# A hand-set order for the first loads and splits of x in a hybrid state-space / convolution step

## The chip, the cores and the metric

The kernel runs on one core of a Trainium2 chip. The metric is the time on the device in microseconds (us); a kernel's time is the median of several executions.

## The reference

The reference is one inference step of a two-layer decoder trunk, for a prompt of 512 tokens and 64 tokens of samples that share all weights. Cut to what matters:

```python
xn = rms_norm(x, norm_mix[0])                  # x: tokens x 1024
proj = xn @ w_in_ab                            # columns z | x,B,C | dt (Mamba-2) and u (S5)
ya = mamba2_mixer(proj[..., :A_PROJ], ...)     # causal conv, chunked scan, gate
yb = s5_mixer(proj[..., A_PROJ:], ...)         # 64 groups of 16 channels, complex diagonal state, GLU
x = x + concatenate([ya, yb]) @ w_out_ab
x = x + square(relu(rms_norm(x, norm_ff[0]) @ w_ff1[0])) @ w_ff2[0]
x = x + conformer_conv_module(rms_norm(x, norm_mix[1]), ...)
x = x + square(relu(rms_norm(x, norm_ff[1]) @ w_ff1[1])) @ w_ff2[1]
y = rms_norm(x, norm_final)                    # all in float32
```

## The kernel before

**Layout.** All 576 tokens run together. x lies with its 1024 channels on the partitions, as eight tiles of 128 x 576 (channels by tokens), named xi0 to xi7. A weight is read in tiles of 128 output columns: one DMA brings 128 x 1024, which holds eight blocks of 128 x 128, one for each tile of x.

**Products.** A float32 product is made of three products of a shorter format: each operand is split into hi (rounded, on ScalarE) and lo (the remainder, on VectorE). `load` (L203 to L213) does so for a weight tile: the DMA is issued on SyncE (L208), hi is written by ScalarE (L211) and lo by VectorE (L212). Its pool has two buffers. `mm` (L215) then issues for each of the eight blocks hi by hi, hi by lo and lo by hi, each for two halves of 288 tokens: 48 matmuls a tile (L226), into one of two PSUM buffers; a buffer (its "bank" below) comes free when the tile has been read out. `split_scaled` (L243) splits x with the norm's weight multiplied in, hi as fxh on ScalarE (L248) and lo as fxl on VectorE (L249).

**The norm.** The scale of each token is not multiplied into x but into the products. `tok_sum` (L263) squares the tiles on ScalarE (L270; the first is named sa, the others sq), adds them up on VectorE (L274) and sums over the channels on TensorE (tsum, L280). `rstd_tok` (L283) makes the scale r on VectorE by three Newton steps (last step L298), and `bcast_tok` (L300) spreads r over the partitions by small matmuls (bc, L310), which ScalarE copies out as rB (L311, L312).

**The first mixer.** `mixer0` (from L1043) loads x (L1051), splits it, makes the norm's scale, then the S5 coefficients (`s5_coef`: many small steps on VectorE, polynomial steps at L418, products at L509) and tables (`s5_in`: kt by TensorE, L559; ks = kt + dm by VectorE, L562; transposes p, L568). Eight tiles of w_in follow, tiles 0 to 7, for the S5 inputs u. Tiles 0 and 1 are copied out raw by ScalarE (ur, L1066); tiles 2 to 7 are read from PSUM by VectorE when it multiplies by rB to make u (`s5_u`, L576), which is written to memory and read back for the state products (s5s, L600). Tile 8 is dt. Then come four groups of six tiles, tiles 9 to 32, for the convolution, the scan and the gate of Mamba-2 (first step on VectorE: xb, L757), while the S5 outputs are made beside them. The output projection follows, whose residual sum is xr (L1138).

**What sets the order.** Each engine works off its own queue in program order and waits for the other engines by semaphores. The order in a queue is made when the kernel is built: a scheduler takes the next instruction by a modelled time line and a priority. `with self.hp(...)` raises the priority of what is recorded inside; `load` is recorded so, with 3000. Of the loads of x only xi0 is raised (4000):

```python
for k in range(8):
    t = self.X("xi%d" % k)
    with self.hp(4000 if k < 1 else 0):
        nc.sync.dma_start(t, I["x"][k])
    x.append(t)
act = [self.split_scaled(x[k], self.v("nm0", k), "fx", self.B) for k in range(8)]
_, rB = self.rms(x, "rB0")
```

Two small loads are issued from ScalarE's own queue: aco, the convolution's state (L727), and adt, the bias and decay of dt (L733).

Of the kernel before, what the change touches and what calls it, by code (L numbers as in the profile page):

```python
# [1 line left out]

# [1 line left out]

# [4 lines left out]
F32 = mybir.dt.float32  # L9
F32R = mybir.dt.float32r  # L10
AF = mybir.ActivationFunctionType
ALU = mybir.AluOpType
# [130 lines left out]
class Build:  # L143
# [46 lines left out]
    def consts(self):  # L190
# [8 lines left out]
        self.ident, self.tri, self.tris, self.same = (c[:, i * 128:(i + 1) * 128] for i in range(4))  # L199
        self.m8, self.md, self.sgn = c[:, 512:520], c[:, 520:536], c[:, 536:537]  # L200


    def load(self, src, eng=None):  # L203
        nc = self.nc
        eng = eng or nc.vector
        with self.hp():
            raw = self.wp.tile([128, 1024], F32, tag="raw", name="raw")
            nc.sync.dma_start(raw, src)  # L208
            hi = self.wp.tile([128, 1024], F32R, tag="hi", name="hi")
            lo = self.wp.tile([128, 1024], F32R, tag="lo", name="lo")  # L210
            nc.scalar.activation(hi, raw, AF.Copy)  # L211
            eng.tensor_tensor(lo, raw, hi.bitcast(F32), op=ALU.subtract)  # L212
        return hi, lo  # L213

    def mm(self, src, act, eng=None, halves=(0, 1)):  # L215

        nc = self.nc
        hi, lo = self.load(src, eng)
        ps = self.pm.tile([128, 2, 512], F32, tag="mm", name="mm")
        n = 0  # L220
        for kb in range(8):
            ah, al = act[kb]
            k = slice(kb * 128, kb * 128 + 128)
            for w, a in ((hi, ah), (hi, al), (lo, ah)):
                for h in halves:
                    nc.tensor.matmul(ps[:, h, :H], w[:, k], a[:, h * H:(h + 1) * H], start=n == 0, stop=n == 23)  # L226
                n += 1
        return ps[:, :, :H]
# [34 lines left out]
    def tok_sum(self, tiles, mk=None, mk2=None, bank=None):  # L263

        nc = self.nc
        mk = mk or (lambda n: self.tp.tile([128, NT], F32, tag="sa", name=n, bufs=1))
        acc = None
        for t in tiles:
            s = ((mk2 or self.t)("sq") if acc is not None else mk("sa"))[:, :t.shape[-1]]
            nc.scalar.activation(s, t, AF.Square)  # L270
            if acc is None:
                acc = s
            else:
                nc.vector.tensor_tensor(acc, acc, s, op=ALU.add)  # L274
        n = acc.shape[-1]
        c, p = n // 128, n % 128
        ps = (bank or self.bank)("tsum")
        for k in range(c + 1):
            m = 128 if k < c else p
            nc.tensor.matmul(ps[:m, k:k + 1], acc[:, k * 128:k * 128 + m], self.ones[:, 0:1], start=True, stop=True)  # L280
        return ps, c, p
# [761 lines left out]
    def mixer0(self):  # L1043
        nc, I = self.nc, self.I
        with self.tc.tile_pool(name="q1", bufs=5) as self.q1, ExitStack() as inner:
            self.qs = inner.enter_context(self.tc.tile_pool(name="qs", bufs=2))
            x = []
            for k in range(8):
                t = self.X("xi%d" % k)
                with self.hp(4000 if k < 1 else 0):  # L1050
                    nc.sync.dma_start(t, I["x"][k])  # L1051
                x.append(t)
            act = [self.split_scaled(x[k], self.v("nm0", k), "fx", self.B) for k in range(8)]
            _, rB = self.rms(x, "rB0")
            self.s5_coef()
            self.a_conv_init()
            self.S = self.qs.tile([128, 72, 2, 32], F32, tag="S", name="S", bufs=1)
# [1 line left out]
            for m in range(2):  # L1059
                P[m] = self.s5_in(m)  # L1060
            for m in range(8):
                ps = self.mm(I["w_in"][m], act)
                if m < 2:
                    t = self.t("ur", "t")
                    with self.hp():
                        nc.scalar.activation(h2(t), ps, AF.Copy)  # L1066
                    ps = h2(t)
# [65 lines left out]
            for m in range(8):  # L1133
                ps = self.mm(I["w_out"][8 + m], act)
# [284 lines left out]
```

## Time and profile before

| | |
|---|---|
| three executions | 1676.21, 1678.60, 1682.48 us |
| median | 1678.6 us |
| profiled execution, its own time | 1674.24 us |
| span of its trace | 1672.5 us |
| TensorE's granted clock, mean over the span | 0.970 of full speed |
| TensorE busy (matmuls) | 1591.3 us, 95% of the span |
| VectorE busy | 1054.5 us, 63% |
| ScalarE busy | 634.8 us, 38% |
| instructions | 28815 |

The durations of the rows come from the one profiled execution. Its own time is 1.74 us longer than its span, and 4.4 us shorter than the median of the three executions. The busy shares are means over the whole span: they say which engine is closest to full, but not which one is waited for in a given stretch. That is read from the timelines, where a row gives start, length, engine, line, operation, output<-inputs, shape, and in square brackets the idle time of the engine just before and what ended it. A row with "x4" stands for four instructions in a row.

### The profile page before, as it was taken

Reading aid. Unit: us, or ns where it says so; the run is one execution under the profiler, and the core shown is the slowest. Engines: PE = TensorE matmul, PEld = TensorE weight load, DVE = VectorE, ACT = ScalarE, POOL = GpSimd, SP = SyncE. Lnnn points to the kernel's source line nnn. Section 1 sums busy time; section 2 is a strip of 40 time slices with the busy share of each in tenths; the row PEclk is TensorE's granted clock in tenths of the full one; section 3 lists DMA queues with packets and bytes.
Section 4 is the critical chain, followed back from the end, with each engine's and each line's share of the span. In section 5 each row is a group of like instructions: output and inputs, shape, how many; then the busy total and the mean of one; then the engine's idle time right before and its main releaser. Section 6 shows DMA issues by size and latency. Waiting matters only on the chain.

```text
span 1672.5 us, 28815 instructions
## 1 busy us (share of the span) xinstructions
PE 1591.3 (95%) x11833; PEld 1557.6 (93%) x11833; DVE 1054.5 (63%) x1796; ACT 634.8 (38%) x1081; POOL 4.7 (0%) x45
## 2 busy tenths in 40 slices
PE   7999889999998999999999999996799999999997
PEld 7999789989897999999999999995799999999996
DVE  7988899876647966754443557587454443444466
ACT  4244556675514333322222353223333222222244
POOL 0000000000000000000000000000000000000000
PEclk9999999999998999999999999997799999999998
DMA  6644457687766434432222245641022222222234
GB/s 197 180 109 132 131 172 197 197 267 220 251 234 188 94 97 129 154 127 78 87 77 88 78 146 148 189 107 30 25 77 77 89 76 89 85 81 88 78 127 132
DMA packets 149883, 214.43 MB, mean 128 GB/s; under 512 B 59034, under 2 KB 94874, under 8 KB 149752
## 3 DMA queue, kind: packets, MB, share of 16 engines
q1 hardware_dynamic: 146088, 211.28, 41.2%
q8 instruction: 93, 1.52, 0.4%
q10 hardware_dynamic: 3664, 1.32, 0.3%
q14 instruction: 38, 0.31, 0.1%
HBM read 181.22 MB, written 31.34 MB: 127 GB/s over the span
## 4 chain that ended last, share of the span: by engine, by line
PE 82%; DVE 7%; DMA 6%; ACT 2%; issue 1%; SPq 1%; ACTq 0%; DVEq 0%
PE mm L226 72%; PE pc L1308 2%; DVE lo L212 1%; DMA sg<-cumd 1%; DMA rl<-yad 1%; PE pc L1374 1%; PE tsum L1216 1%; PE bc L310 1%; DMA rl<-ybd 1%; DMA rl<-yg 1%; PE pt L1259 1%; DMA ud<-u 1%; PE s5s L600 1%; PE s5y L704 0%; PE s5y L705 0%
## 5 line engine op out<-in xcount | busy, mean ns | idle before, releaser
L211 ACT ACTIVATE hi<-raw 128x1024 fp32r<-128x1024 f32 x217 | 229.7, 1060 | 740.2 <-PE mm L226 685.6
L226 PE MATMUL mm<-fxh,hi 128*128 128x288 f32 x1920 | 418.2, 299 | 23.8 <-ACT hi L211 10.4
L212 DVE TENSOR_TENSOR lo<-raw,hi 128x1024 fp32r<-128x1024 f32 x217 | 264.8, 1221 | 259.0 <-ACT hi L211 257.5
L226 PE MATMUL mm<-fxh,lo 128*128 128x288 f32 x1920 | 417.4, 298 | 0.0
L226 PE MATMUL mm<-fxl,hi 128*128 128x288 f32 x1920 | 415.0, 298 | 0.0
L226 PEld LDWEIGHTS mm<-fxh,hi 128*128 128x128 f32 x1920 | 311.7, 190 | 26.7 <-ACT hi L211 12.7
L226 PEld LDWEIGHTS mm<-fxh,lo 128*128 128x128 f32 x1920 | 311.6, 190 | 1.8 <-issue 1.1
L226 PEld LDWEIGHTS mm<-fxl,hi 128*128 128x128 f32 x1920 | 311.9, 190 | 0.4
L226 PE MATMUL mm<-gh,hi 128*128 128x288 f32 x1024 | 230.0, 295 | 0.0
L226 PE MATMUL mm<-gh,lo 128*128 128x288 f32 x1024 | 229.4, 295 | 0.5 <-DVE lo L212 0.5
L226 PE MATMUL mm<-gl,hi 128*128 128x288 f32 x1024 | 229.5, 295 | 0.0
L226 PEld LDWEIGHTS mm<-gh,lo 128*128 128x128 f32 x1024 | 167.5, 188 | 0.8 <-DVE lo L212 0.8
L226 PEld LDWEIGHTS mm<-gl,hi 128*128 128x128 f32 x1024 | 167.9, 188 | 0.0
L226 PEld LDWEIGHTS mm<-gh,hi 128*128 128x128 f32 x1024 | 167.6, 188 | 0.0
L350 DVE TENSOR_TENSOR fft<-mm,r2B 128x576 f32<-128x576 f32 x56 | 42.4, 758 | 140.5 <-PE mm L226 140.5
L1376 DVE SCALAR_TENSOR_TENSOR acc<-hb,vec,acc 128x512 f32<-128x512 f32 x104 | 77.2, 748 | 1.3
L343 DVE TENSOR_TENSOR ffr<-ffr 128x576 f32<-128x576 f32 x64 | 48.5, 758 | 2.3 <-ACT gh L342 0.4
L344 DVE TENSOR_TENSOR gl<-ffr,gh 128x576 fp32r<-128x576 f32 x64 | 48.5, 758 | 2.1
L342 ACT ACTIVATE gh<-ffr 128x576 fp32r<-128x576 f32 x64 | 44.1, 689 | 2.0
L351 DVE TENSOR_TENSOR x<-x,fft 128x576 f32<-128x576 f32 x56 | 42.4, 758 | 1.8
L765 DVE SCALAR_TENSOR_TENSOR cvo<-xb,vh,cvo 128x600 f32<-128x600 f32 x48 | 40.0, 833 | 1.4 <-ACT cvo L763 1.4
L340 ACT ACTIVATE ffr<-mm 128x576 f32<-128x576 f32 x64 | 40.6, 634 | 0.0
(356 smaller groups left out, 1903.1 us busy)
## 6 DMA issues: line engine op xcount, KB each, us to landing
raw<-w_ff SPq DMA_DIRECT2D x136, 512.0 KB, 3.5
raw<-w_in SPq DMA_DIRECT2D x33, 512.0 KB, 3.7
raw<-w_pw SPq DMA_DIRECT2D x24, 512.0 KB, 3.6
dm<-dwm SPq DMA_DIRECT2D x16, 576.0 KB, 5.9
h<-ass SPq DMA_DIRECT2D x16, 512.0 KB, 4.7
raw<-w_out SPq DMA_DIRECT2D x16, 512.0 KB, 4.5
U<-ud SPq DMA_DIRECT2D x16, 288.0 KB, 3.0
xsd<-xs SPq DMA_DIRECT2D x16, 288.0 KB, 4.0
```

Of the source, the lines that this page charges most:

```text
L211: nc.scalar.activation(hi, raw, AF.Copy)
L212: eng.tensor_tensor(lo, raw, hi.bitcast(F32), op=ALU.subtract)
L226: nc.tensor.matmul(ps[:, h, :H], w[:, k], a[:, h * H:(h + 1) * H], start=n == 0, stop=n == 23)
L340: nc.scalar.activation(h2(r), ps, AF.Relu)
L342: nc.scalar.activation(hi, r, AF.Square)
L343: nc.vector.tensor_tensor(r, r, r, op=ALU.mult)
L344: nc.vector.tensor_tensor(lo, r, hi.bitcast(F32), op=ALU.subtract)
L350: nc.vector.tensor_tensor(h2(t), ps, rB, op=ALU.mult)
L351: nc.vector.tensor_tensor(x[m], x[m], t, op=ALU.add)
L765: nc.vector.scalar_tensor_tensor(o[:, 0:600], xb[:, k:k + 600], self.half("acw", 16 * k + m), o[:, 0:600], op0=ALU.mult, op1=ALU.add)
L1308: nc.tensor.matmul(pc[:, g * 128:g * 128 + 128], w[:, j * 128:j * 128 + 128], hq[:, g, j:j + 128], start=j == 0, stop=j == 8)
L1376: nc.vector.scalar_tensor_tensor(ap, hb[:, k:k + NP], w(k), ap, op0=ALU.mult, op1=ALU.add)
```

## The change

The eight tiles of x and of their splits are now taken from their pools first. Then, all with priority 4000, each tile is loaded, rounded on ScalarE and its remainder made on VectorE; the load and the split of weight tile 0 are recorded right behind those of xi0, and `mm` takes this tile as already loaded. The loads are kept as one list (SyncE), the roundings as another (ScalarE) and the remainders as a third (VectorE), with those of weight tile 0 in second place. Behind the list of ScalarE stands the first square, and behind that of VectorE the first add of squares. `chain` ties each instruction of a list to the one ahead of it, as an order for the scheduler, without a semaphore. `tok_sum` keeps its squares and adds for that. What is computed stays the same. (`behind_load`, which is also new, is called nowhere and is left out below; the line numbers of the new kernel are higher by 13 from `load` on and by 22 behind this place in `mixer0`.)

```diff
--- before
+++ after
...
+    def chain(self, ins):
+
+        for a, b in zip(ins, ins[1:]):
+            self.tc.add_manual_dep(b.ins, a.ins.name, mybir.DependencyInfo(mybir.DependencyClass.NoSync, mybir.DependencyReason.DATA),
+                                   reason="chain")
+
...
     def load(self, src, eng=None):
         nc = self.nc
         eng = eng or nc.vector
         with self.hp():
             raw = self.wp.tile([128, 1024], F32, tag="raw", name="raw")
-            nc.sync.dma_start(raw, src)
             hi = self.wp.tile([128, 1024], F32R, tag="hi", name="hi")
             lo = self.wp.tile([128, 1024], F32R, tag="lo", name="lo")
-            nc.scalar.activation(hi, raw, AF.Copy)
-            eng.tensor_tensor(lo, raw, hi.bitcast(F32), op=ALU.subtract)
+            self.last = [nc.sync.dma_start(raw, src), nc.scalar.activation(hi, raw, AF.Copy),
+                         eng.tensor_tensor(lo, raw, hi.bitcast(F32), op=ALU.subtract)]
         return hi, lo
 
     def mm(self, src, act, eng=None, halves=(0, 1)):
 
         nc = self.nc
-        hi, lo = self.load(src, eng)
+        hi, lo = src if isinstance(src, tuple) else self.load(src, eng)
         ps = self.pm.tile([128, 2, 512], F32, tag="mm", name="mm")
         n = 0
         for kb in range(8):
@@ -264,14 +277,14 @@
 
         nc = self.nc
         mk = mk or (lambda n: self.tp.tile([128, NT], F32, tag="sa", name=n, bufs=1))
-        acc = None
+        acc, self.sq = None, ([], [])
         for t in tiles:
             s = ((mk2 or self.t)("sq") if acc is not None else mk("sa"))[:, :t.shape[-1]]
-            nc.scalar.activation(s, t, AF.Square)
+            self.sq[0].append(nc.scalar.activation(s, t, AF.Square))
             if acc is None:
                 acc = s
             else:
-                nc.vector.tensor_tensor(acc, acc, s, op=ALU.add)
+                self.sq[1].append(nc.vector.tensor_tensor(acc, acc, s, op=ALU.add))
         n = acc.shape[-1]
         c, p = n // 128, n % 128
         ps = (bank or self.bank)("tsum")
@@ -1044,14 +1057,23 @@
         nc, I = self.nc, self.I
         with self.tc.tile_pool(name="q1", bufs=5) as self.q1, ExitStack() as inner:
             self.qs = inner.enter_context(self.tc.tile_pool(name="qs", bufs=2))
-            x = []
-            for k in range(8):
-                t = self.X("xi%d" % k)
-                with self.hp(4000 if k < 1 else 0):
-                    nc.sync.dma_start(t, I["x"][k])
-                x.append(t)
-            act = [self.split_scaled(x[k], self.v("nm0", k), "fx", self.B) for k in range(8)]
+
+            x = [self.X("xi%d" % k) for k in range(8)]
+            act = [(self.B("fxh", F32R), self.B("fxl", F32R)) for k in range(8)]
+            q = [[], [], []]
+            with self.hp(4000):
+                for k in range(8):
+                    q[0].append(nc.sync.dma_start(x[k], I["x"][k]))
+                    q[1].append(nc.scalar.activation(act[k][0], x[k], AF.Copy, scale=self.v("nm0", k)))
+                    q[2].append(nc.vector.scalar_tensor_tensor(act[k][1], x[k], self.v("nm0", k), act[k][0].bitcast(F32),
+                                                               op0=ALU.mult, op1=ALU.subtract))
+                    if k == 0:
+                        w0 = self.load(I["w_in"][0])
+                        for a, b in zip(q, self.last):
+                            a.append(b)
             _, rB = self.rms(x, "rB0")
+            for a, b in zip(q, ([], self.sq[0], self.sq[1])):
+                self.chain(a + b[:1])
             self.s5_coef()
             self.a_conv_init()
             self.S = self.qs.tile([128, 72, 2, 32], F32, tag="S", name="S", bufs=1)
@@ -1059,7 +1081,7 @@
             for m in range(2):
                 P[m] = self.s5_in(m)
             for m in range(8):
-                ps = self.mm(I["w_in"][m], act)
+                ps = self.mm(I["w_in"][m] if m else w0, act)
                 if m < 2:
                     t = self.t("ur", "t")
                     with self.hp():
```

The scheduler then orders the rest anew, so more moves than the diff names. Three places follow.

**The start, ScalarE and TensorE.** fxh is the rounding of a tile of x (xi_90 is xi0 in both; then every second number before, every number after, up to xi7), hi that of a weight tile, sq and sa the squares; aco and adt are the small loads. ScalarE before, from the load adt on:

```order
L727 DMA aco<-acs 128x16x24
L733 DMA adt<-adt 128x32
L211 ACTIVATE hi<-raw 128x1024 x2
L248 ACTIVATE fxh<-xi_92,vec 128x576
L270 ACTIVATE sq<-xi_92 128x576
L754 ACTIVATE xb<-aco 128x8x3
L248 ACTIVATE fxh<-xi_94,vec 128x576
L270 ACTIVATE sq<-xi_94 128x576
L827 ACTIVATE ea<-adt 128x16
L248 ACTIVATE fxh<-xi_96,vec 128x576
```

ScalarE in the new order, from the same load on:

```order
L746 DMA adt<-adt 128x32
L224 ACTIVATE hi<-raw 128x1024
L1067 ACTIVATE fxh<-xi_91,vec 128x576
L283 ACTIVATE sq<-xi_91 128x576
L1067 ACTIVATE fxh<-xi_92,vec 128x576
L283 ACTIVATE sq<-xi_92 128x576
L767 ACTIVATE xb<-aco 128x8x3
L1067 ACTIVATE fxh<-xi_93,vec 128x576
L283 ACTIVATE sq<-xi_93 128x576
L840 ACTIVATE ea<-adt 128x16
L1067 ACTIVATE fxh<-xi_94,vec 128x576
L1067 ACTIVATE fxh<-xi_95,vec 128x576
```

Weight tile 1's rounding, which stood with tile 0's in the row "x2", has moved behind all roundings of x; xi6 and xi7 follow the last row shown, then sa, the square of xi0, and then two weight tiles. The loads aco and adt stand ahead of the first weight rounding in both.

TensorE's first rows before; mm_526 is tile 0 and mm_659 tile 1:

```order
L226 MATMUL mm_659<-fxh_106,hi_655 128x288 x2
L226 MATMUL mm_659<-fxl_107,hi_655 128x288 x2
L226 MATMUL mm_526<-fxh_110,hi_522 128x288 x2
L226 MATMUL mm_659<-fxh_106,lo_656 128x288 x2
L226 MATMUL mm_659<-fxh_110,hi_655 128x288 x2
L226 MATMUL mm_526<-fxl_111,hi_522 128x288 x2
L226 MATMUL mm_526<-fxh_110,lo_523 128x288 x2
```

and in the new order, at the same rows:

```order
L239 MATMUL mm_526<-fxh_100,hi_118 128x288 x2
L239 MATMUL mm_526<-fxl_101,hi_118 128x288 x2
L239 MATMUL mm_526<-fxh_100,lo_119 128x288 x2
L239 MATMUL mm_526<-fxh_102,hi_118 128x288 x2
L239 MATMUL mm_526<-fxl_103,hi_118 128x288 x2
L239 MATMUL mm_526<-fxh_102,lo_119 128x288 x2
L239 MATMUL mm_526<-fxh_104,hi_118 128x288 x2
```

Tile 1 was woven into tile 0; now it starts in row 25, when all rows of tile 0 are done.

**VectorE around r.** r is the norm's scale; the rows at L418 before are polynomial steps of the S5 coefficients, those at L509 (L522 after) products. Before:

```order
L296 TENSOR_TENSOR rs<-ry 128x5
L418 SCALAR_TENSOR_TENSOR wr_195<-wr_195,wr_196 128x96 x2
L418 SCALAR_TENSOR_TENSOR wr_196<-wr_196 128x96
L297 TENSOR_TENSOR rs<-rs,rv 128x5
L418 SCALAR_TENSOR_TENSOR wr_195<-wr_195,wr_196 128x96 x2
L418 SCALAR_TENSOR_TENSOR wr_196<-wr_196 128x96
L298 SCALAR_TENSOR_TENSOR r_167<-rs,ry 128x5
L289 MEMSET rv 128x1
L418 SCALAR_TENSOR_TENSOR wr_195<-wr_195,wr_196 128x96 x2
L434 SCALAR_TENSOR_TENSOR mag<-wr_195,ei 128x96
```

In the new order:

```order
L309 TENSOR_TENSOR rs<-ry 128x5
L487 TENSOR_TENSOR AR<-pw 128x96
L522 TENSOR_TENSOR wr_202<-wr_202 128x96
L522 TENSOR_TENSOR wr_201<-wr_202,wr_201 128x96
L490 TENSOR_TENSOR pw<-AI,AR 128x96
L522 TENSOR_TENSOR wr_201<-wr_201 128x96
L310 TENSOR_TENSOR rs<-rs,rv 128x5
L485 TENSOR_TENSOR pw<-AR 128x192
L426 TENSOR_SCALAR wr_202<-wr_202 128x96
L491 TENSOR_TENSOR AI<-pw 128x96
L311 SCALAR_TENSOR_TENSOR r_173<-rs,ry 128x5
```

r has moved from row 81 to row 114: the steps of the S5 coefficients that stand ahead of it are more, and include the reciprocal and the first powers (pw, AR, AI), which stood behind it. bc follows tile 2 and stands ahead of tile 3 in TensorE's queue in both orders.

**VectorE around u.** u of tiles 0 and 1 is made from ur, that of tile 2 from the PSUM bank mm, which comes free by it. Before:

```order
L212 TENSOR_TENSOR lo<-raw,hi 128x1024
L455 SCALAR_TENSOR_TENSOR wr_195<-wr_196 128x96
L418 SCALAR_TENSOR_TENSOR wr_195<-wr_195,wr_196 128x96
L576 TENSOR_TENSOR u<-ur,rB_185 128x72x8
L509 TENSOR_TENSOR wr_195<-wr_195 128x96
L509 TENSOR_TENSOR wr_196<-s5c 128x96
L418 SCALAR_TENSOR_TENSOR wr_195<-wr_195,wr_196 128x96
L576 TENSOR_TENSOR u<-ur,rB_185 128x72x8
L413 TENSOR_SCALAR wr_196<-wr_195 128x96
L418 SCALAR_TENSOR_TENSOR wr_195<-wr_195 128x96
L509 TENSOR_TENSOR wr_196<-s5c 128x96
L576 TENSOR_TENSOR u<-mm,rB_185 128x72x8
```

In the new order:

```order
L589 TENSOR_TENSOR u<-ur,rB_191 128x72x8
L487 TENSOR_TENSOR AR<-pw 128x384
L491 TENSOR_TENSOR AI<-pw 128x384
L566 TENSOR_TENSOR bb<-bb,bt 128x128
L589 TENSOR_TENSOR u<-ur,rB_191 128x72x8
L507 TENSOR_SCALAR L_318<-AR 128x32 x2
L564 TENSOR_TENSOR bs<-by,kr 128x128
L507 TENSOR_SCALAR L_318<-AI 128x32 x2
L508 TENSOR_SCALAR AI<-AI,cst 128x9x64
L565 TENSOR_TENSOR bt<-bx,kis 128x128
L547 TENSOR_TENSOR G<-AR,bb 128x1024
L589 TENSOR_TENSOR u<-mm,rB_191 128x72x8
```

u of tile 2 stood in row 98, 17 rows behind r; it now stands in row 143, 29 rows behind r, with the powers of A (L485 to L491 of the new kernel) and the first product for G (L547) ahead of it.

## Rows read from the trace of the kernel before

**Rows 1.** The page: busy us, share of the span and instructions of each engine
```profile
PE 1591.3 (95%) x11833; PEld 1557.6 (93%) x11833; DVE 1054.5 (63%) x1796; ACT 634.8 (38%) x1081; POOL 4.7 (0%) x45
```

**Rows 2.** Stretches: start:end, length, busy PE, PEld, DVE, ACT, POOL; granted clock, DMA share, GB/s
```profile
150.00:290.00 140.00, 124.06 (x930) 119.32 (x930) 133.87 (x280) 78.03 (x179) 1.07 (x9) 0.94 0.54 161
290.00:400.00 110.00, 105.54 (x839) 100.01 (x838) 83.09 (x159) 73.80 (x187) 0.20 (x2) 0.97 0.77 234
```

**Rows 3.** ScalarE's timeline: start us, us, engine line op, out<-in [idle before <-releaser]
```profile
5.05 4.18 ACTq L733 DMA_DIRECT2D adt<-adt  x1
...
9.27 2.00 ACT L211 ACTIVATE hi<-raw 128x1024 fp32r<-128x1024 f32 x2 [2.39 <-issue]
...
16.59 0.76 ACT L248 ACTIVATE fxh<-xi,vec 128x576 fp32r<-128x576 f32 x1
...
17.26 0.67 ACT L270 ACTIVATE sq<-xi 128x576 f32<-128x576 f32 x1
```

**Rows 4.** SyncE's timeline, the last seven loads of x
```profile
2.12 6.99 SPq L1051 DMA_DIRECT2D xi<-x  x7
```

**Rows 5.** TensorE's timeline, at twelve places of the first 270 us
```profile
10.38 0.85 PE L226 MATMUL mm<-fxh,hi 128*128 128x288 f32 x2 [10.38 <-ACT hi L211]
...
14.69 0.69 PE L226 MATMUL mm<-fxl,hi 128*128 128x288 f32 x2
...
15.17 0.69 PE L226 MATMUL mm<-fxh,lo 128*128 128x288 f32 x2
...
17.14 0.43 PE L226 MATMUL mm<-fxh,lo 128*128 128x288 f32 x2
...
17.41 0.42 PE L226 MATMUL mm<-fxl,hi 128*128 128x288 f32 x2
...
25.94 1.15 PE L280 MATMUL tsum<-ones,sa 128*128 128x1 f32 x10
...
33.98 1.52 PE L310 MATMUL bc<-cst,r 128*128 128x128 f32 x10 [0.15 <-DVE rv L289]
...
36.48 0.53 PE L226 MATMUL mm<-fxh,hi 128*128 128x288 f32 x2 [0.98 <-ACT ur L1066]
...
42.98 0.42 PE L226 MATMUL mm<-fxh,hi 128*128 128x288 f32 x2
...
80.24 0.66 PE L568 MATMUL p<-cst,G 128*128 128x128 f32 x4 [2.59 <-DVE ks L562]
...
131.93 0.38 PE L226 MATMUL mm<-fxh,lo 128*128 128x288 f32 x1
...
263.93 0.51 PE L226 MATMUL mm<-fxh,hi 128*128 128x288 f32 x2
```

**Rows 6.** VectorE's timeline, at seven places up to 486 us
```profile
33.77 0.15 DVE L298 SCALAR_TENSOR_TENSOR r<-rs,ry 128x5 f32<-128x5 f32 x1
...
34.53 0.25 DVE L418 SCALAR_TENSOR_TENSOR wr<-wr,wr 128x96 f32<-128x96 f32 x1
...
34.70 1.22 DVE L212 TENSOR_TENSOR lo<-raw,hi 128x1024 fp32r<-128x1024 f32 x1
...
39.36 1.32 DVE L576 TENSOR_TENSOR u<-mm,rB 128x576 f32<-128x576 f32 x1
...
130.84 0.29 DVE L562 TENSOR_TENSOR ks<-kt,dm 128x128 f32<-128x128 f32 x1 [4.65 <-PE kt L559]
...
264.68 0.21 DVE L757 TENSOR_TENSOR xb<-mm,rB 128x64 f32<-128x64 f32 x1
...
485.32 0.76 DVE L1138 TENSOR_TENSOR xr<-mm,xr 128x576 f32<-128x576 f32 x1 [1.99 <-PE mm L226]
```

**Rows 7.** Stretches of 2 us, columns as in rows 2: the first matmuls, and 80 to 84
```profile
14.00:16.00 2.00, 2.00 (x10) 2.00 (x10) 2.00 (x7) 1.40 (x4) 0.00 (x0) 1.00 0.98 317
...
80.00:82.00 2.00, 1.76 (x11) 1.74 (x12) 2.00 (x4) 0.60 (x1) 0.00 (x0) 0.71 0.56 130
...
82.00:84.00 2.00, 2.00 (x11) 1.65 (x11) 1.99 (x3) 0.81 (x2) 0.00 (x0) 0.50 0.93 298
```

More of the change, by code (lines that the diff above doesn't have):

```diff
@@ L1 @@
-from contextlib import ExitStack
+from contextlib import ExitStack, contextmanager
 import numpy as np
@@ L200, in consts, with behind_load @@
         self.m8, self.md, self.sgn = c[:, 512:520], c[:, 520:536], c[:, 536:537]
+    def chain(self, ins):
+        for a, b in zip(ins, ins[1:]):
+            self.tc.add_manual_dep(b.ins, a.ins.name, mybir.DependencyInfo(mybir.DependencyClass.NoSync, mybir.DependencyReason.DATA),
+                                   reason="chain")
+    @contextmanager
+    def behind_load(self):
+        with ExitStack() as st:
+            for i in self.last:
+                st.enter_context(self.tc.issue_after(i.ins))
+            yield
     def load(self, src, eng=None):
```

## The prediction, made before the result was known

> **What bounds the kernel now.** I read the page's busy shares first, then the stretches, then the timelines of the engines over the first 50 us and at a few later points. TensorE is busy 95% of the span [rows 1], so an edit wins only where TensorE stands still or runs slowly, and loses by adding such places. One such place is the start: the first matmul comes at 10.38 us [rows 5]. Another is 150 to 290 us: TensorE is busy 124.1 of 140 us and VectorE 133.9 [rows 2]. There VectorE sets the pace, and TensorE stands still for 15.9 us.
>
> The start is held by ScalarE. The issue of the small load adt stands in its queue from 5.05 to 9.23, and only behind it does the first weight split run, 9.27 on [rows 3]. TensorE then has work without a gap until the sums of squares at 25.94 [rows 5].
>
> **The start after the change.** The squares and w1 go behind the x splits, but adt's issue stays ahead of the first weight split on ScalarE, as the order shows. So the first matmul stays at 10.4 and the loads in front gain nothing there. SyncE issued the last x before 9.11 [rows 4] and now does so one weight issue sooner; ScalarE reaches those tiles later anyway, so I cost that at nothing. If ScalarE were free sooner, the same loads would be what it waits for next.
>
> Before, tiles 0 and 1 of w_in were woven together; now tile 0 runs alone. ScalarE does seven more roundings and three squares, 0.67 us start to start [rows 3], before x7 is rounded: 10.3 + 10 times 0.67 and two short steps give about 17.5. VectorE's remainder of x7 follows at about 19.2, and tile 0 ends at 19.8. Tile 1 then waits for its own weight remainder, which VectorE does behind all x remainders: 20.3 plus 1.2 [rows 6] gives 21.5, and 44 matmuls at 0.134 [rows 5] end at 27.4 against 25.94. That is **1.5 us late**.
>
> Here the clock is to be weighed. The matmuls before 16 us stand 0.24 us apart, those behind 0.134 [rows 5]; 288 columns make 0.24 at 1.2 GHz and 0.12 at 2.4. I let the slow pace stay for the same stretch, since TensorE stood idle before it in both kernels. But the granted clock reads 1.00 there [rows 7]; if that is right and the pace is only the weave waiting for splits, tile 0 alone loses it and 24 times 0.106 = 2.5 us come back. The Trainium skill (TensorE: Matmul & The Clock Gate, section "What's actually happening") puts it so: "the default state is throttled, and activity releases the throttle"; by that page nothing comes back, and the sum stands without it.
>
> **The step that I think decides: the row scale.** The scale r of the first norm is written on VectorE at 33.77 before [rows 6], just as TensorE ends tile 2, and its broadcast bc starts at 33.98 [rows 5]. In the new order 107 VectorE instructions lie from the first weight remainder to r, where there were 73. The 34 more are one weight remainder (1.2), 7 polynomial steps (0.17 each start to start, as from 34.53 to 34.70 [rows 6]), 11 products of the same size, a reciprocal (0.7) and 14 of 0.1 to 0.3: about 7.2 us. VectorE waits a little for tile 3's split and for the sums there, as it did before for a split, so r comes at 41.0.
>
> bc stands in TensorE's queue ahead of tile 3 in both orders. Tile 2 with the sums (1.1 us) ends at 27.4 + 6.4 + 1.1 = 34.9, so TensorE stands still about 6 us. From bc to tile 3 it took 36.48 - 33.98 = 2.5 us [rows 5], because ScalarE empties tile 1's bank only behind the broadcast; tile 3 starts at 43.6. Tile 4 needs tile 2's bank, which u frees. That u began at 39.36 [rows 6]; the new order puts 12.0 us more of VectorE's work ahead of it (the 7.2, then the powers of A and the first product for G). It ends at 39.36 + 12.0 + 1.3 = 52.7, and tile 4 starts there, against 42.98 [rows 5]: **9.7 us late**. Every tile of w_in behind it is late with it.
>
> **What comes back.** VectorE does the S5 coefficients in that time, so the small S5 matmuls (kt, p2, s5s) now run between tiles 4 to 8 and not behind them. Before, TensorE needed 131.93 - 42.98 = 88.95 us [rows 5] from tile 4 until nearly all of these and three conv tiles (9 to 11) were done, 2.6 of it a wait for ks [rows 5]. Without that wait and the three tiles (144 matmuls at 0.134 = 19.3) the work is 67.0. In the new order it is done at 52.7 + 67.0 = 119.7, and with the three tiles at 139.0, against 131.93: **7 us late** is left. VectorE's last S5 step stood at 130.84, behind a wait of 4.65 [rows 6]; it now has two conv tiles less ahead of it (some 10 us), so it is done by about 115, and the late side is TensorE.
>
> Then comes the stretch where VectorE sets the pace. TensorE's 7 us could vanish in its 15.9 us of standing still [rows 2], which gives 0. Against that: when VectorE had done its work up to 264.68 (xb of tile 24) [rows 6], TensorE was starting tile 26, at 263.93 [rows 5]. In the new order, with as much work done on VectorE, TensorE starts tile 23. Three tiles less and 1.4 us more of small matmuls: 17.9 us of TensorE's work have left VectorE's shadow. VectorE comes to that point at about 258 (the same work less 1.6, and some 5 us less waiting, as the 4.65 goes). The rest took 485.32 - 264.68 = 220.6 us [rows 6]; it grows by about 20 for that work and shrinks by about 6, for a late TensorE no longer meets the last wait before 290 nor most of the 4.5 us at 290 to 400 [rows 2]. 258 + 220.6 + 20 - 6 = 492.6 against 485.3: +7. From there on the order differs in detail only, and I count nothing.
>
> The ends of this step are 0 and +10 (if VectorE does not wait less). I take **+7**, the end that counts the work row by row and that agrees with the lateness at 131.93. Against the profiled execution (1674.24) that is 1681. The median of the runs is 1678.6, 4.4 above it, and 1678.6 + 7 = 1685.6, so I say 1685. About 0.5% (8.4 us) is what a measurement of this kernel can tell from no change.
>
> **Rivals.**
> Slower: the same late r, but nothing is repaid. The two gaps between 35 and 53 each put the array on the lower clock: after the wait of 2.59 us that ends at 80.24 [rows 5] the granted clock is 0.71 and 0.50 until 84 [rows 7], 1.6 us lost each time, 3.2 for both. And VectorE waits again for a kt, which now stands near the end of tile 7's matmuls: 4.65, as before [rows 6]. 10 + 3.2 + 4.65 = +18, so 1696. It decides from the point where TensorE still stands still 13 us or more at 150 to 290. For it: VectorE's queue order is fixed, so r cannot come sooner. Against: a VectorE that runs on while TensorE is late has less left to do.
>
> Faster: TensorE's 15.9 us of standing still vanish, because S5 is off VectorE 15 us sooner: 7 - 15.9 = -8.9, so 1670, or 1667 if the 2.5 us of the slow start come back too. For it: VectorE is the pacer there. Against: two conv tiles are merely moved behind.
>
> No effect: the change does not do what it says, since adt and not the loads holds the first matmul, and the late r is swallowed whole by later waits: 1679. For it: 15.9 us of waits are more than 9.7.
>
> **How the numbers follow.** Forecast (+7) 0.40, slower rival 0.32, faster 0.12, no effect 0.16. Four fifths of the forecast's own spread (+2 to +10) lie within the bound. So faster 0.12, same 0.16 + 0.32 = 0.48, slower 0.32 + 0.08 = 0.40. The range runs from the faster rival, 1667, to 3 us above the slower one, 1699.
>
> **What would show it.** Right: first matmul at 10.2 to 10.6; sums of squares at 31 to 33; bc at 40 to 42 with TensorE idle about 6 us ahead of it; tile 4 at 51 to 55; the last kt before 120; granted clock under 1 between 35 and 60. Wrong at the first step if the first matmul comes before 9.5, at the second if bc starts before 37, at the third if TensorE stands still less than 6 us at 150 to 290, which would make the kernel faster.

## The result: 16.6 us slower, and the profile after

| | before | after |
|---|---|---|
| median of 6 runs, us | 1683.0 | 1698.5 |
| lowest and highest, us | 1676.2, 1684.9 | 1695.3, 1701.5 |
| ratio to before | | 1.0099 [1.0076, 1.0123] |
| profiled execution, span, us | 1672.5 | 1699.7 |
| granted clock, mean of the span | 0.970 | 0.955 |

The changed kernel is 1.0% slower; on the 1678.6 us of the prediction that is +16.6 us, for a forecast of +7. (The ratio is one of means; the two medians differ by 15.5 us.) The two profiled executions lie at opposite ends of their kernels' runs, so their spans differ by 27.2 us: I use them to find places, and the ratios for sizes.

The page after, its line on busy engines, beside [rows 1]:

```profile
PE 1606.4 (95%) x11833; PEld 1571.7 (92%) x11833; DVE 1056.1 (62%) x1796; ACT 634.0 (37%) x1081; POOL 4.6 (0%) x45
```

TensorE has the same 11833 matmuls, but is busy 1606.4 - 1591.3 = 15.1 us longer. It also stands still longer: 1699.7 - 1606.4 = 93.3 us for 1672.5 - 1591.3 = 81.2. So about half of the difference of the spans is standing still, and about half is matmuls that run slower. Both have places. TensorE's timeline after, at the start:

```profile
9.89 0.85 PE L239 MATMUL mm<-fxh,hi 128*128 128x288 f32 x2 [9.89 <-ACT hi L224]
...
15.16 0.68 PE L239 MATMUL mm<-fxl,hi 128*128 128x288 f32 x2
...
15.64 0.47 PE L239 MATMUL mm<-fxh,lo 128*128 128x288 f32 x2
...
30.80 1.15 PE L293 MATMUL tsum<-ones,sa 128*128 128x1 f32 x10
...
40.70 2.69 PE L323 MATMUL bc<-cst,r 128*128 128x128 f32 x10 [5.90 <-DVE rv L302]
...
44.25 0.85 PE L239 MATMUL mm<-fxh,hi 128*128 128x288 f32 x2 [0.86 <-ACT ur L1088]
```

and VectorE's, with the scale r, the u of tile 2, and the two waits for kt (columns of both as in [rows 3]):

```profile
40.48 0.17 DVE L311 SCALAR_TENSOR_TENSOR r<-rs,ry 128x5 f32<-128x5 f32 x1
...
50.60 1.32 DVE L589 TENSOR_TENSOR u<-mm,rB 128x576 f32<-128x576 f32 x1
...
111.64 0.29 DVE L575 TENSOR_TENSOR ks<-kt,dm 128x128 f32<-128x128 f32 x1 [5.23 <-PE kt L572]
...
119.67 0.29 DVE L575 TENSOR_TENSOR ks<-kt,dm 128x128 f32<-128x128 f32 x1 [2.79 <-PE kt L572]
```

bc comes at 40.70 behind 5.90 us of standing still, for 0.15 in [rows 5], since VectorE writes r at 40.48 and not at 33.77 [rows 6]. Then stretches of after, columns as in [rows 2]:

```profile
0.00:267.80 267.80, 231.44 (x1669) 223.13 (x1670) 231.53 (x527) 125.35 (x269) 1.34 (x15) 0.91 0.54 153
...
39.00:50.00 11.00, 8.44 (x34) 8.03 (x35) 11.00 (x42) 1.36 (x3) 0.24 (x2) 0.53 0.27 74
...
150.00:290.00 140.00, 124.56 (x924) 119.30 (x923) 132.99 (x272) 79.46 (x184) 0.90 (x9) 0.90 0.58 167
...
380.00:401.00 21.00, 16.50 (x82) 16.24 (x81) 15.01 (x28) 12.31 (x25) 0.00 (x0) 0.52 0.78 240
...
527.00:545.00 18.00, 11.05 (x43) 10.04 (x44) 13.06 (x18) 6.68 (x10) 0.15 (x1) 0.53 0.80 203
```

and of before, the first 264.68 us and the last two of these:

```profile
0.00:264.68 264.68, 236.53 (x1788) 229.45 (x1789) 231.48 (x531) 126.69 (x272) 1.56 (x17) 0.97 0.54 156
...
380.00:401.00 21.00, 21.00 (x158) 20.35 (x157) 12.14 (x26) 13.73 (x35) 0.00 (x0) 0.92 0.79 234
...
527.00:545.00 18.00, 14.71 (x94) 13.84 (x93) 14.70 (x16) 6.22 (x8) 0.15 (x1) 0.91 0.37 89
```

The granted clock is 0.53 of full speed in the 11 us around the late bc, 0.52 and 0.53 in the two later stretches, where before it was 0.92 and 0.91 (the same time, somewhat later work). Each such stretch has a wait in it or just ahead of it. TensorE's waits after, summed up over the first 600 us (what waits, what for: us in all, times, longest; without the wait for the first weight):

```profile
PE mm L239 <- ACT yah L261: 12.7, 4, 5.6
...
PE yps L937 <- DVE ya L949: 8.6, 2, 8.2
...
PE yoff L979 <- DMA h<-ass: 6.0, 3, 4.5
...
PE bc L323 <- DVE rv L302: 5.9, 1, 5.9
...
PE cum L850 <- DVE da L842: 4.4, 1, 4.4
```

and before:

```profile
PE scr L898 <- ACT bt L890: 4.6, 1, 4.6
...
PE mm L226 <- DVE z L779: 4.1, 1, 4.1
...
PE tsum L280 <- DVE sa L274: 3.1, 1, 3.1
...
PE p L568 <- DVE ks L562: 2.6, 1, 2.6
...
PE mm L226 <- ACT yah L248: 2.6, 3, 1.2
```

The waits have changed names. Of those after, only the one for r (rv) lies in the first 50 us; the others come behind 165 us, in code that the diff does not touch. Three of them in TensorE's timeline of after:

```profile
228.69 1.12 PE L937 MATMUL yps<-sg,xd 128*64 128x128 f32 x8 [8.20 <-DVE ya L949]
...
388.15 3.56 PE L979 MATMUL yoff<-xs,h 128*128 128x8 f32 x16 [4.50 <-DMA h<-ass]
...
535.73 1.80 PE L239 MATMUL mm<-yah,hi 128*128 128x288 f32 x4 [5.57 <-ACT yah L261]
```

### The profile page after: what moved, and what is told of

It reads as the page before. It is cut to its first block, busy times and chain, and to the rows that moved or that the text cites. A ratio compares the mean times of both kernels' runs of the same rounds, so it can differ in the third digit from the quotient of the medians.

```text
span 1699.7 us, 28792 instructions
## 1 busy us (share of the span) xinstructions
PE 1606.4 (95%) x11833; PEld 1571.7 (92%) x11833; DVE 1056.1 (62%) x1796; ACT 634.0 (37%) x1081; POOL 4.6 (0%) x45
## 4 chain that ended last, share of the span: by engine, by line
PE 84%; DMA 6%; DVE 6%; issue 1%; SPq 1%; ACT 1%; DVEq 0%; ACTq 0%
PE mm L239 73%; PE pc L1330 2%; DMA h<-ass 1%; PE yoff L979 1%; DVE lo L225 1%; PE pc L1396 1%; PE bc L323 1%; PE s5y L717 1%; PE s5y L718 1%; PE tsum L1238 1%; DMA rl<-yad 1%; SPq L592 1%; DMA sg<-cumd 1%; PE tsum L293 1%; DMA adt<-adt 1%
## 5 line engine op out<-in xcount | busy, mean ns | idle before, releaser
L239 PE MATMUL mm<-fxl,hi 128*128 128x288 f32 x1920 | 420.3, 300 | 0.0
L239 PE MATMUL mm<-yah,hi 128*128 128x288 f32 x128 | 30.3, 322 | 14.6 <-ACT yah L261 12.7
```

## Experiments

Most runs change the order alone. They take the code of before (so its line numbers) and a method that ties every instruction of an engine to the one ahead of it in a given list, without a semaphore, as `chain` does. Nothing but the order differs from before.

```diff
+    def pin(self):
+        at = {i.name: i for i in self.nc.cur_bb.bb.instructions}
+        for names in ORDER:
+            for a, b in zip(names, names[1:]):
+                self.tc.add_manual_dep(at[b], a, mybir.DependencyInfo(mybir.DependencyClass.NoSync, mybir.DependencyReason.DATA), reason="pin")
...
+        self.pin()
```

Below, the list is written in words (in the runs it stands packed, as numbers). A cut "at 50 us" is made on all engines at the places that stand in the trace about there. In the expectations tile 8 (dt) is not counted, so a tile k from 9 on is tile k+1 of the kernel. All ratios are to before, run on the same chip. Before's own median is 1676.3 to 1678.4 us beside these runs and was 1683.0 beside the changed kernel, so I read no difference of 0.3% between ratios from different chips.

**Is it the late row scale?** Three lists:

```diff
-ORDER = before
+ORDER = changed to 50 us, before behind
```

> The kernel before with every engine's order written out by hand: the first stretch (on VectorE up to u of tile 2, on TensorE up to the end of tile 3, the like on ScalarE and SyncE) as in the changed kernel, and everything behind it as in the kernel before. Theory 'head' (the late row scale r and the late u of tile 2 cost the time, and nothing behind repays it): the row scale's broadcast at about 41, tile 4 at about 53, and 13 to 17 us slower than before. Theory 'tail' (what costs is the order behind 50 us, which puts S5 work on VectorE ahead of the w_in tiles): tile 4 just as late, but the 10 us are mostly swallowed by later waits, 0 to 5 us slower than before.

1685.9 us, 1.0037 [1.0020, 1.0055]. Tile 4 starts at 53.61, 10.6 us late, and the profile ends 11.3 us late. By the ratio 3 to 9 us of that stay lost (6 in the middle, between what the two theories expected). So a late r does cost time when before's order stands behind it.

```diff
-ORDER = before
+ORDER = before to 50 us, changed behind
```

> The other half: the first stretch as in the kernel before, everything behind it in the order of the changed kernel. Theory 'head': r at 33.8, tile 4 at 43, within 3 us of before. Theory 'tail': the same start, but TensorE waits at 130 to 240 us as in the changed kernel, 10 to 17 us slower than before.

1698.5 us, 1.0118 [1.0101, 1.0135]: no late start, and the whole loss, more than either theory expected. Tile 4 starts at 43.45, and this is what follows on TensorE:

```profile
56.56 3.59 PE L559 MATMUL kt<-cm,G 128*128 128x16 f32 x16 [9.49 <-DVE G L536]
```

TensorE comes to the first kt 9.5 us before VectorE has made G. The third list repeats that without a cut:

```diff
 ORDER = changed
-VectorE: 11 steps of r and 3 of u behind the powers of A
+VectorE: 11 steps of r and 3 of u ahead of them
```

> The order of the changed kernel on all engines with 14 VectorE instructions moved forward: the steps of the row scale r stand together right behind the sums, and u of tiles 0, 1 and 2 stand where their inputs come in. Theory 'head': the broadcast at 35 instead of 41, tile 4 at 44 instead of 53, and the kernel within 4 us of before. Theory 'tail': the start is mended in the same way, but 6 to 12 us slower than before are left.

1698.7 us, 1.0120 [1.0097, 1.0144]. r is written at 34.43, and TensorE does this:

```profile
44.22 0.50 PE L226 MATMUL mm<-fxh,hi 128*128 128x288 f32 x2 [0.22 <-DVE AR L474]
...
57.09 3.17 PE L559 MATMUL kt<-cm,G 128*128 128x16 f32 x14 [9.19 <-DVE G L536]
```

Tile 4 starts at 44.22 for 53.23, but TensorE loses the 9 us 13 us later: VectorE has the same work ahead of G as without the move, and r early only moves the place at which TensorE waits for it. The late row scale is there as forecast, and taking it away gains nothing in the changed order. The step that I thought decides does not decide.

**Is it the ties, or the new order behind them?**

```diff
-            for a, b in zip(q, ([], self.sq[0], self.sq[1])):
-                self.chain(a + b[:1])
+            for a in q:
+                self.chain(a)
```

> The changed kernel without the tie of the first square and the first add behind the splits: the loads and the splits of x keep their fixed order, the scheduler places the squares. r stands in VectorE's row 90 instead of 117, and 16 tiles of w_in stand ahead of the decay sums of Mamba-2 on TensorE (18.6 before, 14.7 in the changed kernel). Theory 'head': r as early as before, within 4 us of before. Theory 'tail': between the two, 5 to 12 us slower than before.

1690.6 us, 1.0077 [1.0056, 1.0098].

```diff
-            for a, b in zip(q, ([], self.sq[0], self.sq[1])):
-                self.chain(a + b[:1])
```

> The changed kernel with none of the ties; the loads and splits of x and of weight tile 0 are only recorded in front with the high priority. On TensorE the S5 products kt stand behind 6.5 tiles, the decay sums of Mamba-2 behind 15.9 (before 7.2 and 18.6, changed kernel 4.5 and 14.7). If the place of these sums among the tiles is what costs: 5 to 12 us slower than before. If the ties themselves cost: within 3 us of before.

1687.5 us, 1.0061 [1.0044, 1.0079].

```diff
-                with self.hp(4000 if k < 1 else 0):
+                with self.hp(4000):
```

> The kernel before with one number changed: all eight loads of x have the priority that xi0 has. No ties, no early split of weight tile 0. kt stands behind 5.5 tiles, the decay sums behind 15.5. If the place of these sums among the tiles is what costs: 7 to 15 us slower than before. If the ties or the early split cost: within 3 us of before.

The last is before with one number changed, the priority of the loads of x: 1704.9 us, 1.0166 [1.0150, 1.0181], the slowest of the three. Its first matmul comes late,

```profile
21.38 0.85 PE L226 MATMUL mm<-fxh,hi 128*128 128x288 f32 x2 [21.38 <-ACT hi L211]
```

but 11 us at the start are not the 28 us by which it is longer. No tie is needed, then: with each of these edits the scheduler sorts what is behind the start anew, and the kernel loses 0.6 to 1.7%. With all ties the loss is 0.99%, without them 0.61%; the intervals overlap, so whether the ties add anything is not shown.

**Where behind the start?** Cuts at later places, first with the changed order in front:

```diff
-ORDER = before
+ORDER = changed to 153 us, before behind
```

> The other half: up to the start of tile 12 (153 us) as in the changed kernel, behind it as in the kernel before. Theory 'S5 stretch': 8 to 17 us slower than before. Theory 'scan stretch': tile 12 is 10 to 12 us late as in the changed kernel, but S5 is further on than before, so 0 to 6 us slower.

1686.5 us, 1.0057 [1.0041, 1.0072].

```diff
-ORDER = before
+ORDER = changed to 257 us, before behind
```

> The order of the changed kernel up to 257 us, where TensorE is 47 us behind before in tiles of w_in, and the order of before behind it. Theory 'early' (what is missing when VectorE's stretch ends at some 300 us is lost): VectorE's order of before hands out the missing tiles one after another, TensorE cannot make up all of them, 8 to 16 us slower than before. Theory 'late' (the order behind 314 us is what costs): 3 to 9 us slower, as with the cut at 153 us.

1699.0 us, 1.0136 [1.0113, 1.0158].

```diff
-ORDER = before
+ORDER = changed to 314 us, before behind
```

> The order of the changed kernel up to 314 us, the order of before behind it. Theory 'early': the two tiles that are missing at 300 us are not made up, 12 to 20 us slower than before. Theory 'late': 0 to 9 us slower.

1686.1 us, 1.0053 [1.0037, 1.0069].

```diff
-ORDER = before
+ORDER = changed to 314 us with r early, before behind
```

> The kernel with the changed order and the row scale moved forward, up to 314 us, and the order of before behind it. The same cut with the late row scale was 0.53% (9 us) slower than before. If the late row scale makes that part: 0 to 3 us slower than before. If it is hidden there too, as in the whole changed order: 6 to 12 us slower.

1687.1 us, 1.0055 [1.0033, 1.0076].

```diff
-ORDER = before
+ORDER = changed to 460 us, before behind
```

> The order of the changed kernel up to 460 us (the w_glu tiles done), the order of before behind it. If the waits for ya at 527 to 550 us are what the later order costs: 6 to 11 us slower than before (0.4 to 0.65%), near the cut at 314 us. If the scan's last steps at 380 to 400 us are: 13 to 18 us slower, near the whole changed order.

1690.3 us, 1.0084 [1.0063, 1.0104].

So 0.53% (9 us) of the loss is there with the cut at 314 us, with r late or early, 0.84% (14 us) at 460, and the whole has 0.99%. TensorE's waits up to 600 us with the cut at 314:

```profile
PE yps L924 <- DVE ya L936: 9.0, 2, 8.2
...
PE bc L310 <- DVE rv L289: 5.9, 1, 5.9
...
PE mm L226 <- ACT yah L248: 3.2, 4, 1.6
```

and at 460:

```profile
PE yps L924 <- DVE ya L936: 9.2, 2, 8.2
...
PE yoff L966 <- DMA h<-ass: 6.7, 2, 6.1
...
PE mm L226 <- ACT yah L248: 3.8, 5, 1.2
```

The wait of 8.2 for ya (at 228 us) is in both. A long wait for h, the scan's state that is read back from memory, appears only with the cut at 460 (with the cut at 314 it is 1.0 us in all). In the changed kernel its load is issued at 383.68, when TensorE has just run out of work (383.65): the 4.50 us ahead of 388.15 above. The 12.7 us for the splits of ya, at 527 to 551, are there only in the whole change: 3.2 and 3.8 in these two. The cut at 257 does not fit into the row and costs more than 314. The cuts from the other side show what may be behind that.

```diff
-ORDER = changed
+ORDER = before to 141 us, changed behind
```

> Every engine's order written out: up to the start of tile 12 (141 us) as in the kernel before, behind it as in the changed kernel. Two theories on where the changed order costs. Theory 'S5 stretch' (tiles 4 to 11: TensorE's queue asks for the S5 products kt after 4.5 tiles instead of 7.2, VectorE cannot deliver them so soon, and the conv tiles come late): 0 to 4 us slower than before. Theory 'scan stretch' (tiles 12 to 48: what is put on VectorE ahead of the conv steps makes TensorE stand still at 130 to 240 us and run at half the clock behind each stop): 12 to 20 us slower than before.

1700.5 us, 1.0138 [1.0122, 1.0153].

```diff
-ORDER = changed
+ORDER = before to 210 us, changed behind
```

> As the kernel with the order of before up to tile 12 and of the changed one behind it, but with the order of before up to 210 us (tile 20). Theory 'tiles in VectorE's shadow': what is lost between tiles 12 and 20 is not lost here, and 23 us shrink to 5 to 12 us slower than before. Theory 'late stretch' (the waits for h at 388 us and for ya at 525 to 550 us are the cause): 18 to 24 us slower than before, as with the cut at tile 12.

1707.1 us, 1.0180 [1.0149, 1.0210].

```diff
-ORDER = changed
+ORDER = before to 286 us, changed behind
```

> The same with the cut at 286 us (tile 26). Theory 'tiles in VectorE's shadow': 0 to 6 us slower than before. Theory 'late stretch': 18 to 24 us slower.

1706.5 us, 1.0172 [1.0148, 1.0196].

```diff
-ORDER = changed
+ORDER = before to 398 us, changed behind
```

> The order of before up to 398 us, the order of the changed kernel behind it: on VectorE the w_glu tiles come later among the scan's last steps (38 tiles instead of 40 when VectorE has done 400 us of work), and the splits of ya stand as in the changed kernel. Theory 'early': only the longer waits at the start of the last projection are left (some 5 us in the profiles), 1 to 6 us slower. Theory 'late': 10 to 20 us slower.

1707.4 us, 1.0178 [1.0151, 1.0205]. All four have higher ratios than the whole change, the last three beyond the intervals, and lose more (23 to 30 us) than any theory expected. The last one runs with before up to the cut, and then its TensorE does this:

```profile
400.43 3.55 PE L966 MATMUL yoff<-xs,h 128*128 128x8 f32 x16 [5.22 <-DMA h<-ass]
...
409.05 2.14 PE L280 MATMUL tsum<-ones,sa 128*128 128x1 f32 x10 [5.06 <-DVE sa L274]
...
413.69 5.28 PE L310 MATMUL bc<-cst,r 128*128 128x128 f32 x20 [2.50 <-DVE rv L289]
```

Before has none of these waits here. Work that one order has left for later and the other has done sooner comes at once behind a cut. A cut has a price of its own, so the pieces do not add up, and what a cut shows may be more than what the order in front of it costs. The 0.53% at 314 us may hold such a price too.

The kernels without a cut need no such allowance. The profiles tell when TensorE starts its n-th matmul; the table has by how many us later than in the profile of before. (The order is another, so the matmuls ahead of the n-th are not quite the same ones: differences of 2 or 3 us are not read. The last row is before's own order on TensorE, in the run adt_behind_the_start below, and shows how much another execution moves these numbers.)

| n-th matmul | 2100 | 2500 | 2700 | 3500 | 4000 | 8000 | last |
|---|---|---|---|---|---|---|---|
| before starts it at, us | 308.1 | 359.7 | 388.2 | 497.6 | 579.1 | 1111.4 | 1665.3 |
| changed kernel | +11.6 | +9.4 | +17.5 | +16.6 | +25.2 | +25.0 | +27.2 |
| no ties (no_chain) | -1.8 | -4.1 | +9.5 | +7.4 | +10.2 | +10.1 | +12.5 |
| squares not tied (chain_without_squares) | -2.0 | -4.3 | +9.3 | +6.6 | +13.3 | +13.1 | +14.6 |
| changed to 460 us | +8.3 | +5.8 | +14.8 | +16.8 | +17.4 | +18.0 | +20.9 |
| changed to 314 us | +4.4 | +5.8 | +8.7 | +8.9 | +9.4 | +9.5 | +11.3 |
| order of before | +1.9 | +2.0 | +5.8 | +5.7 | +5.3 | +5.3 | +5.9 |

Two places stand out. Between the 2500th and the 2700th matmul, where TensorE waits for h (4.5 us in the changed kernel, 2.8 without ties), the kernels with the changed order there lose 8 to 14 us, those with before's order 3 or 4. Between the 3500th and the 4000th, where it waits for the splits of ya, the first three lose 3 to 9 us, and the three with before's order there nothing. The two kernels with fewer ties are on time at 308 us: they lose only behind it.

**Would a TensorE that is early in the stretch at 150 to 290 us keep its lead?** Three small changes to before's order.

```diff
 ORDER = before, at 200 to 216 us
-VectorE: S5 scan steps, then three cvo, xs, z;  ScalarE: sg, xw, then bt, hi
+VectorE: three cvo, xs, z, then S5 scan steps;  ScalarE: bt, hi, then sg, xw
```

> The kernel before with its order written out, and at one place (200 to 216 us) changed: on VectorE the conv taps cvo, the step xs and the gate step z, which gives a PSUM bank back to TensorE, stand ahead of S5 scan steps instead of behind them; on ScalarE the copies bt and the next weight rounding stand ahead of xw and sg. No amount of work changes. Theory 'tiles in VectorE's shadow' (the time depends on how many w_in tiles TensorE has done for the same work of VectorE, so the changed kernel loses by putting scan steps ahead of conv steps): the waits of 4.6 and 4.1 us at 203 and 210 go, and the kernel is 2 to 7 us faster than before. Rival 'VectorE's work alone' (VectorE paces the stretch, and the order of its steps does not matter): within 2 us of before.

1678.6 us, 1.0002 [0.9988, 1.0016]. A tile starts at 205.75 for 210.41, 4.7 us early:

```profile
205.75 0.85 PE L226 MATMUL mm<-fxh,hi 128*128 128x288 f32 x2 [4.30 <-DVE z L779]
...
244.97 0.67 PE L705 MATMUL s5y<-P,hm 128*72 128x128 f32 x2 [3.98 <-ACT cvo L763]
```

By 271 us it is 2.4 late. What was gained is waited for again, each time for VectorE or ScalarE, so the first theory falls here.

```diff
 ORDER = before
-ScalarE: issue of aco, adt, then the first weight rounding
+ScalarE: the first weight rounding; the issues and their two readers at 36 us
```

> The kernel before with its order written out, and on ScalarE the issues of the small loads aco and adt and the two steps that read them moved behind the start (to 36 us). If the start counts one for one: the first matmul comes at 7 to 8 instead of 10.4, tiles 0 and 1 end 1 to 3 us sooner, and the kernel is 1 to 3 us faster. If the row scale or the loads of x are the next limit: tile 4 at 43 as before, within 1 us of before.

1676.5 us, 0.9995 [0.9980, 1.0009].

```profile
8.25 0.85 PE L226 MATMUL mm<-fxh,hi 128*128 128x288 f32 x2 [8.25 <-ACT hi L211]
...
81.29 1.11 PE L568 MATMUL p<-cst,G 128*128 128x128 f32 x4 [4.12 <-DVE ks L562]
```

The issues of aco and adt did hold the first matmul: 8.25 for 10.38. The 2 us are still there at tile 7 and go at 81.29 in a wait for ks, 4.12 us for 2.59.

```diff
-ORDER = before
+ORDER = that of chain_without_squares to 138 us, before behind
```

> Up to 138 us (tile 12) the order of the kernel whose squares are not tied, which at that point was 3.3 us ahead of before, VectorE by 6 us; behind it the order of before. If the time is VectorE's lead plus the tiles that TensorE has done: 2 to 5 us faster than before. If later waits swallow the lead: within 2 us of before.

1676.9 us, 1.0002 [0.9989, 1.0015]. The first part of that kernel is as good as before's; its 0.77% come from behind 138 us, as the table above has it. No version was faster than before by more than its interval.

## Why the prediction had the sign and not the size

**The start: right, to 0.7 us.** First matmul 9.89 (forecast 10.2 to 10.6; one weight rounding stands ahead of it, not two), sums 30.80 (31 to 33), r 40.48 (41.0), 5.90 us idle ahead of bc (about 6), tile 3 at 44.25 (43.6), tile 4 at 53.23 (52.7). Counting instructions in the new queue at durations from rows gave a place 53 us into the program to half a microsecond. The matmuls stand 0.24 us apart until 15.64 and closer behind it, as the forecast let them; tile 0 runs alone, so the weave was not the cause, though the granted clock reads 1.00 there. By its pace, not by that reading, the trace agrees with what the forecast quotes from the Trainium skill (TensorE: Matmul & The Clock Gate, section "What's actually happening").

**What comes back: this step failed.** Forecast: tile 12 at 139.0 against 131.93, 7 us late. Measured: 146.66 against 132.15, 14.5 late. And "VectorE comes to that point at about 258 (the same work less 1.6, and some 5 us less waiting, as the 4.65 goes)": it needed 231.48 us of work up to 264.68 before, and has done as much, 231.53, at 267.80 after (the stretches above), 9.8 us later than forecast. Its last S5 step, forecast for about 115, starts at 119.67. The wait for kt did not go. VectorE's waits after, 50 to 268 us,

```profile
DVE ks L575 <- PE kt L572: 8.9, 3, 5.2
```

and before, 40 to 265:

```profile
DVE ks L562 <- PE kt L559: 6.2, 3, 4.7
```

I took 4.65 off 6.2 and got 8.9: 7.4 of the 9.8 us. The slower rival had this ("VectorE waits again for a kt"), and the clock: 0.53 at 39 to 50, where the forecast took full speed. Its condition held too: TensorE still stands still 15.4 us at 150 to 290 (15.9 before). Its +18 is nearer to the 16.6 than my +7.

The late r is not what makes these 9.8 us. With r early VectorE has done as much work at 265.6, and its waits in this stretch read, in part:

```profile
DVE ks L562 <- DMA dm<-s5d: 3.3, 1, 3.3
...
DVE ks L562 <- PE kt L559: 2.6, 2, 2.4
```

Its last ks comes at 118.55 for 119.67: what it waits less for kt it waits in part for the small load dm, and the kernel is no faster.

Nor do the 9.8 us explain the whole miss. The forecast's sum ended at 492.6 for the row of VectorE at 485.32, the fifth of the eight residual sums. After, that row reads

```profile
508.26 0.75 DVE L1160 TENSOR_TENSOR xr<-mm,xr 128x576 f32<-128x576 f32 x1
```

22.9 us late in the pair of profiles, not 7. From VectorE's point to there "220.6 + 20 - 6" was to be 234.6 us, and is 240.5. The tiles that were to leave VectorE's shadow did leave it: up to that point TensorE has started 159 matmuls of w_in fewer (1067 for 1226, 3.3 tiles for a forecast of 3). But the stretch was taken over from before with no new wait in it. And without the ties VectorE comes to the same amount of work at 260.4, near the forecast's 258; the kernel is slower all the same.

**The cause: "the order differs in detail only, and I count nothing".** Both the forecast and the slower rival put the loss into one late step. Shown by the runs: it is not r (1.0118 and 1.0120 without its lateness); the ties are not needed (1.0061 without them, 1.0166 with one number changed); and waits for h at 388 and for the splits of ya at 527 to 551 us, which before does not have or has shorter, come with the pieces of order that hold them, in kernels that are on time at 308 us too. In the changed kernel TensorE is 11.6 us late at 308 us, not far from the +7. Then come 8.1 around the wait for h, 8.6 around the splits of ya and 2.2 behind 1111 us (the table), in profiles whose spans differ by 10.6 us more than the timing. The forecast had no term for any of these three. Nor had the slower rival, so that its +18 lies near the result is in part luck. The price of such a wait is more than its length. Around the 4.50 that ends at 388.15 the granted clock is 0.62 at 380 to 384, 0.50 from 384 to 400 and 1.00 again from 404: 12 us of matmuls behind the wait ran at half speed.

**Left open.** How the 16.6 us divide between standing still and slow matmuls (12.1 and 15.1 in the pair of profiles, which is 10 more than the timing), which single steps before 314 us make the 0.53%, and what part of it is the price of the cut. That moving the load of h or the splits of ya alone would give the time back was not tried. The steps from 314 to 460 and from there to the end differ by 0.31 and 0.15%, less than their intervals together.

**The rivals of no loss.** "Faster" fell: VectorE was busy 132.99 of 140 us at 150 to 290, as before (133.87), although S5 was to be out of its way. "No effect" fell for the whole, but its thought, that a late start is swallowed by later waits, is true within the changed order; with before's order behind it, 3 to 9 us of the late start stay.

## What to carry to other kernels

An edit at the start of a kernel whose order is made by a scheduler is an edit of the whole order: compare the waits of all stages by name, before and after, and do not stop at the stage that the diff names. To find out whether the edit or the new order costs the time, pin the order of every engine and put the two orders together at a cut, in both directions; but a cut has its own price, so trust a cut that shows no loss more than one that does. Where another engine sets the pace, 2 to 5 us won by TensorE in or ahead of that stretch were gone at the end; of 10 us lost ahead of it, 3 to 9 stayed.

## What the runs showed of the hardware

A wait on TensorE costs more than its length: the same 11833 matmuls were busy 15.1 us longer when the mean granted clock was 0.955 for 0.970, and three stretches near half speed, the lower of the clock's two levels, lie around waits of 3.9 to 5.9 us (0.53 at 39 to 50, 0.52 at 380 to 401, 0.53 at 527 to 545). The clock can fall ahead of the wait: it reads 0.97 at 380 to 381 and 0.50 from 381 on, the wait begins at 383.65, and until then TensorE ran yoff products of 8 columns without a gap; what lowered it was not tried. And the record does not always show the pace: it reads 1.00 at 9.89 to 15.64, with matmuls 0.24 us apart, and they stand as far apart where it reads 0.50, at 44.90 to 49.

The issue of a small load from ScalarE's queue held it 3.69 us (adt, 128 x 32), and 4.18 before [rows 3]. With this issue and that of aco moved to 34 us, where adt's took 1.26 us, the first matmul came 2.1 us sooner.
